# Head of a seven-product output stage: sums moved from GpSimd to VectorE, joint loads of y, loads of weights behind the last copy

## The chip, the cores and the metric

The kernel runs on one core of one Trainium2 chip. The metric is device time in microseconds for one execution; the time before is 2018.6 us, the median of three runs (2017.74 to 2028.34). The names of the engines in views and text: PE is TensorE, DVE is VectorE, ACT is ScalarE, POOL is GpSimd, SP is SyncE; SPq and ACTq are the DMA queues that SP and ACT issue on.

## The reference, cut to what matters

The kernel computes one layer of a hybrid backbone (a gated DeltaNet mixer and a windowed attention mixer) on 2048 latent tokens of width 1024, with 256 context tokens as a prefix. The change lies in its last step, the merge of the two branches and the output projection:

```python
def _merge(ya, yb, ga, gb, w_proj_a, w_proj_b, w_out):
    y = jax.nn.sigmoid(ga) * (ya @ w_proj_a) + jax.nn.sigmoid(gb) * (yb @ w_proj_b)
    return y @ w_out
...
    x = x + gate[:, None] * _merge(ya, yb, ga, gb, w_proj_a, w_proj_b, w_out)
```

`y` is 2048 x 1024, `w_out` is 1024 x 1024, the output is 2048 x 1024 in float32.

## The kernel before, in words

Everything is float32, and each matrix product is made of three passes: an operand is split into a high part of reduced precision (a copy by ACT, a CAST in the profile) and a low part (the operand less its high part, a subtraction on DVE or POOL), and PE adds high x high, low x high and high x low.

**The projections (`project`, `load_y`).** The tokens lie in four groups of 512. For each group the attention and DeltaNet outputs are loaded (`yr`, L1210), copied to `yh` by ACT (L1211) and their low parts `yl` made by DVE (L1212). Then, for each of eight slices m of the width, PE makes two products of 12 matmuls (`pps`, L1229 to L1231), DVE multiplies each by its gate (`ta`, `tb`, L1237, whose gates are loaded from `gasp` and `gbsp` into two buffers each), the two are added (L1239: POOL for the first three groups, DVE for the last) and the sum is stored to `ysp` (L1240) by SP. The last group is index 3. PSUM holds eight banks (`acc`), which go to whichever product comes next as they come free.

**The seven-product stage.** The output projection takes y in eight units of 256 tokens, each a 2 x 2 arrangement of blocks A11, A12, A21, A22 (A's first index is the half of 128 tokens, its second the half of 512 channels), and `w_out` in four quarters B11, B12, B21, B22 of 512 x 512. Each unit takes seven products in place of eight: P1 = A11 B11, P2 = A12 B21, P3 = S4 B22, P7 = S3 T3, P6 = S2 T2, P5 = S1 T1, P4 = A22 T4, with S3 = A11 - A21, S2 = A22 - S3, S4 = A12 - S2, S1 = S2 + A11 on the side of y, and on the side of the weights T3 = B22 - B12 (L1342), T2 = T3 + B11 (L1344), T1 = B22 - T2 (L1457) and T4 = B21 - T2 (L1474). Each product is 12 matmuls (L1434 to L1436). The sums overwrite an operand: T3 stands in B12's tile, T2 in B11's, T1 in B22's, T4 in B21's. Low parts then take over tiles that are done with: T2's that of B12, T1's that of B11, T4's that of B22.

PE's order is the list `seq`: for the first two units each product is made for both units in turn (P1 of unit 0, P1 of unit 1, P2 of unit 0, ...), since the weights' sums are being made then; from unit 2 on it goes unit by unit. Position k in `seq` is the loop's counter. For a position k the high part `ah` (L1319) is made by `his(k)` on ACT and the low part `al` (L1323) by `los(k)`, on DVE, or on POOL for P4. `split_lo` makes the weights' low parts (L1309, 128x2048, on DVE but for T4, which POOL makes).

**What sets the order.** Inside `manual_schedule` DVE, ACT, POOL (and PE in the second block) run in the order in which the code is written, each engine waiting in that order. DMAs are issued on ACT's queue (`adma`: the quarters of `w_out`, L1297, and the blocks of y, L1304) and on SP's (`dma`: x, the gate row `gbc`, the outputs), in order as well; a DMA issue waits until its buffer is free, and the completion semaphores, eight in number, are given to the DMAs of both queues in turn, so that an issue also waits for the earlier DMA on its own semaphore. `issue_after(last["yh", 2])` holds the first loads until the copy of the third y tile of group 3 has been issued; there are four such copies.

The outputs (`outputs(k)`, run one position behind the products) add products into `held` and `hold2` tiles on DVE (L1403 to L1425), `store` multiplies by the gate row (L1389) and adds x (L1390, POOL but for unit 7) and stores.

## Time and profile before

| what | value |
|---|---|
| median of 3 runs | 2018.6 us |
| profiled execution | 2021.32 us |
| its span, first to last instruction | 2019.4 us |
| PE busy | 1923.7 us (95%) |
| DVE busy | 1501.3 us (74%) |
| ACT busy | 807.4 us (40%) |
| POOL busy | 713.7 us (35%) |
| mean granted TensorE clock | 0.984 |

In the timelines a row gives start, duration, engine, line, operation, output<-inputs, shape, and how many alike are merged (x2). A bracket at the end gives how long the engine had been idle before and what released it. "issue" as releaser means that the engine's own queue was busy, with DMA issues for instance. In the rows of waits stand the waiting engine and line, what it waited for, and the total in us, how often, and the longest. Matmuls overlap: their starts are 0.23 us apart at full clock, whatever the duration shown.

### The profile page before, as it was taken

To read this page: it belongs to the slowest core of one execution; us is meant where nothing else is said; L and a number is where in the kernel's file an instruction comes from. 1 tells how busy PE (TensorE), PEld (TensorE's weight loads), DVE (VectorE), ACT (ScalarE), POOL (GpSimd) and SP (SyncE) were. 2 spreads that over 40 slices of the span, in tenths; PEclk is the share of its full clock that TensorE was granted. 3 is DMA by queue.
4 is the path that set the end of the run, shared out by engine and by line. 5 is a ranking of instruction groups with operands and counts; after the bars stand their busy time and mean duration, and the time that the engine had idled before them with its cause. 6 is when DMAs were issued, how large, how long until landed. Compare 5 with 4: busy or idle time off the path is not lost. (4 is left out here: it accounts for less than half of the span.)

```text
span 2019.4 us, 32107 instructions
## 1 busy us (share of the span) xinstructions
PE 1923.7 (95%) x10947; PEld 1611.3 (80%) x10947; DVE 1501.3 (74%) x2863; ACT 807.4 (40%) x1998; POOL 713.7 (35%) x776
## 2 busy tenths in 40 slices
PE   6999999989999999999999999999989999997898
PEld 3888888779998778787888888888778887875786
DVE  6979766667776999999677775536677778657667
ACT  5755545554443322111222232325665656432211
POOL 1742211224542211004222243324555444414675
PEclk8999999999999999999999999999999999998999
DMA  7552326755546633528977777673455645363444
GB/s 259 165 141 85 96 88 159 198 147 157 151 146 181 175 115 110 146 85 234 242 232 225 227 231 210 169 215 116 159 183 159 193 152 178 99 222 110 150 158 130
DMA packets 387831, 333.12 MB, mean 165 GB/s; under 512 B 84120, under 2 KB 307664, under 8 KB 387028
## 3 DMA queue, kind: packets, MB, share of 16 engines
q1 hardware_dynamic: 352244, 288.60, 49.5%
q10 hardware_dynamic: 35424, 42.48, 6.0%
q8 instruction: 87, 1.43, 0.3%
q14 instruction: 76, 0.62, 0.1%
HBM read 220.28 MB, written 109.13 MB: 163 GB/s over the span
## 5 line engine op out<-in xcount | busy, mean ns | idle before, releaser
L524 PE MATMUL rps<-hh,wh 128*128 128x512 f32 x768 | 308.7, 402 | 4.4 <-DVE rt L818 3.2
L526 PE MATMUL rps<-hh,wl 128*128 128x512 f32 x768 | 308.7, 402 | 0.0
L525 PE MATMUL rps<-hl,wh 128*128 128x512 f32 x768 | 307.1, 400 | 0.0
L563 DVE SCALAR_TENSOR_TENSOR cacc<-y,cw,cacc 128x512 f32<-128x512 f32 (+1 forms) x224 | 161.2, 741 | 22.8 <-ACT cacc L561 18.6
L524 PEld LDWEIGHTS rps<-hh,wh 128*128 128x128 f32 x768 | 145.3, 189 | 39.5 <-DVE rt L818 4.0
L524 PE MATMUL lps<-hh,wh 128*128 128x512 f32 (+1 forms) x448 | 171.5, 383 | 0.3 <-ACT y L634 0.3
L525 PEld LDWEIGHTS rps<-hl,wh 128*128 128x128 f32 x768 | 145.4, 189 | 32.6
L525 PE MATMUL lps<-hl,wh 128*128 128x512 f32 (+1 forms) x448 | 171.3, 382 | 0.0
L526 PE MATMUL lps<-hh,wl 128*128 128x512 f32 (+1 forms) x448 | 171.2, 382 | 0.0
L526 PEld LDWEIGHTS rps<-hh,wl 128*128 128x128 f32 x768 | 145.3, 189 | 32.4
L945 DVE TENSOR_TENSOR pl<-pt,ph 128x512 fp32r<-128x512 f32 x156 | 105.4, 685 | 44.4 <-ACT ph L943 43.7
L943 ACT CAST ph<-pt 128x512 fp32r<-128x512 f32 x156 | 90.2, 585 | 109.5 <-PE pt L941 77.0
L917 DVE CUSTOM_DVE_ANT_0 pr<-sc,band,sk 128x640 f32<-128x640 f32 (+1 forms) x128 | 106.6, 862 | 32.6 <-PE sc L913 16.6
L816 ACT ACTIVATE rt<-rps 128x512 f32<-128x512 f32 x96 | 57.2, 596 | 172.2 <-PE rps L526 155.1
L749 DVE TENSOR_TENSOR N<-N,btmp 128x62 f32<-128x62 f32 (+30 forms) x124 | 118.6, 957 | 3.0
L927 POOL TENSOR_SCALAR pr<-pr,sm 128x640 f32<-128x640 f32 (+1 forms) x128 | 99.3, 795 | 55.1 <-DVE sm L925 38.6
L747 DVE TENSOR_TENSOR btmp<-N 128x62 f32<-128x62 f32 (+30 forms) x124 | 115.6, 932 | 3.1
L919 ACT ACTIVATE pr<-pr,sm 128x640 f32<-128x640 f32 (+1 forms) x128 | 104.0, 815 | 20.0 <-DVE sm L917 20.0
L1229 PE MATMUL pps<-yh,wph 128*128 128x512 f32 x256 | 104.6, 412 | 5.2 <-ACT yh L1211 3.6
L245 POOL TENSOR_SCALAR wh<-wr 128x512 fp32r<-128x512 f32 x72 | 48.9, 693 | 169.7 <-PE lps L525 92.7
L246 DVE TENSOR_TENSOR wl<-wr,wh 128x512 fp32r<-128x512 f32 x120 | 90.9, 771 | 23.2 <-POOL wh L245 20.9
L1231 PE MATMUL pps<-yh,wpl 128*128 128x512 f32 x256 | 100.9, 396 | 0.0
(370 smaller groups left out, 5067.1 us busy)
## 6 DMA issues: line engine op xcount, KB each, us to landing
wr<-in_w_in_dram SPq DMA_DIRECT2D x120, 256.0 KB
kw<-Ksp SPq DMA_DIRECT2D x28, 384.0 KB
x<-vsp SPq DMA_DIRECT2D x36, 256.0 KB
k<-ksp SPq DMA_DIRECT2D x34, 256.0 KB
kT<-kTsp SPq DMA_DIRECT2D x34, 256.0 KB
wm<-in_w_mod_dram SPq DMA_DIRECT2D x16, 512.0 KB
xt<-in_x_dram SPq DMA_DIRECT2D x16, 512.0 KB
dtl<-Dsp SPq DMA_DIRECT2D x32, 256.0 KB
```

The source lines that it names most:

```text
L524: T.matmul(ps, lhsT=wh[:, k], rhs=xh[:, k], start=k == 0, stop=False)
L525: T.matmul(ps, lhsT=wh[:, k], rhs=xl[:, k], start=False, stop=False)
L526: T.matmul(ps, lhsT=wl[:, k], rhs=xh[:, k], start=False, stop=k == kt - 1)
L563: V.scalar_tensor_tensor(a, y[:, t:t + n], cw[:, m, t:t + 1], a, op0=ALU.mult, op1=ALU.add)
L747: V.tensor_tensor(tv, A[:, m + 1:, m].unsqueeze(2).to_broadcast([h1 + n, r, m]), A[:, m, 0:m].unsqueeze(1).to_broadcast([h1 + n, r, m]), o ...
L749: V.tensor_tensor(A[:, m + 1:, 0:m], A[:, m + 1:, 0:m], tv, op=ALU.add)
L917: V.tensor_tensor_reduce(s_, ps[:, o:768], band[:, b0:b0 + W + 256], -0.125, sk[:, 1, hd:hd + 1], ALU.add, ALU.min, sm[:, h, 1:2])
L919: S.activation(s_, s_, AF.Exp, scale=-1.0, bias=sm[:, h, 1:2], accum_out=sm[:, h, 2:3])
L927: G.tensor_scalar(p[:, h, :W + 256], p[:, h, :W + 256], sm[:, h, 3:4], 1.0, op0=ALU.mult, op1=ALU.mult)
L945: V.tensor_tensor(pl, pt, f32(ph), op=ALU.subtract)
L1229: T.matmul(ps, lhsT=wh[:, k, ms], rhs=hs[k], start=k == 0, stop=False)
L1231: T.matmul(ps, lhsT=wl[:, k, ms], rhs=hs[k], start=False, stop=k == 3)
```

## The change

1. The first loads of the stage (all four quarters of `w_out`, three blocks of y) are held until the fourth y copy of group 3 has been issued, where it was the third.
2. A21 and A22 of a unit, the two blocks of its second 128 tokens, come in one load of 512 KB into one tile, in place of two loads of 256 KB.
3. The sums S3, S2, S1 of units 0 and 1, the sums of weights T1 and T4, and T4's low part go from POOL to DVE, and DVE's instructions are written in the order in which PE needs them. Unit 2's S3, S2, S4 are made on DVE in one go at position 11, S1 on POOL.
4. The first output block of units 0 and 1 is held and stored at position 9; its multiplication by the gate is on POOL for unit 0 too.
5. From unit 2 on, the loads of the next unit are issued one position earlier (at i == 0).

The core of the diff:

```diff
         def load_quad(u, nm):
             gi, o = units[u]
-            r, c = int(nm[1]) - 1, int(nm[2]) - 1
+            if nm == "A2":
+                t = p4.tile([128, 8, 128], F32, name="yA2", tag=f"yA2{u % 2}")
+                adma(t, ysp[gi][:, :, o + 128:o + 256])
+                Y[u, "A21"], Y[u, "A22"] = t[:, 0:4], t[:, 4:8]
+                return
+            c = int(nm[2]) - 1
...
-            with tc.issue_after(last["yh", 2].ins):
+            with tc.issue_after(last["yh", 3].ins):
                 load_w("B11")
...
-            gp = V if u in (0, 7) else G
+            gp = V if u == 7 else G
...
-                store(u, "00", og, gp)
+                if u < 2:
+                    early[u] = og, G
+                else:
+                    store(u, "00", og, gp)
...
-            for q in ((0, "A21"), (0, "A22"), (1, "A12"), (1, "A21"), (1, "A22")):
+            for q in ((0, "A2"), (1, "A12"), (1, "A2")):
                 load_quad(*q)
...
             los(2)
-            s3(0)
-            s2(0, G)
             his(3)
             los(3)
             split_lo("B22", V)
-            s3(1)
-            s2(1, G)
+            s3(0, V)
+            s2(0, V)
             s4(0)
             his(4)
-            G.tensor_tensor(B["B22"], B["B22"], B["B11"], op=ALU.subtract)
             for k in range(len(seq) + 1):
                 u, i = divmod(k, 7)
-                if i == 1 and 2 <= u < 7:
-                    for nm in ("A11", "A12", "A21", "A22"):
+                if i == 0 and 2 <= u < 7:
+                    for nm in ("A11", "A12", "A2"):
                         load_quad(u + 1, nm)
                 if k + 4 < len(seq):
                     los(k + 4)
                 if k == 0:
                     S.copy(hi["T2"], B["B11"])
+                    s3(1, V)
+                    s2(1, V)
                     s4(1)
                 elif k == 1:
                     split_lo("T3", V, "B12")
-                    s1(0)
-                    s1(1)
-                elif k == 2:
+                elif k == 3:
                     split_lo("T2", V, "B11", "B12")
-                    G.tensor_tensor(B["B21"], B["B21"], B["B11"], op=ALU.subtract)
-                elif k == 3:
+                    V.tensor_tensor(B["B22"], B["B22"], B["B11"], op=ALU.subtract)
+                elif k == 4:
                     S.copy(hi["T1"], B["B22"])
-                elif k == 4:
-                    split_lo("T1", V, "B22", "B11")
+                    s1(0, V)
+                    s1(1, V)
+                    V.tensor_tensor(B["B21"], B["B21"], B["B11"], op=ALU.subtract)
                 elif k == 5:
                     S.copy(hi["T4"], B["B21"])
-                    split_lo("T4", G, "B21", "B22")
+                    split_lo("T1", V, "B22", "B11")
                 elif k == 7:
-                    for nm in ("A11", "A12", "A21"):
-                        load_quad(2, nm)
-                elif k == 8:
-                    load_quad(2, "A22")
+                    split_lo("T4", V, "B21", "B22")
+                    load_quad(2, "A11")
+                    load_quad(2, "A12")
+                elif k == 9:
+                    load_quad(2, "A2")
+                    for u in range(2):
+                        store(u, "00", *early[u])
+                elif k == 11:
+                    s3(2, V)
+                    s2(2, V)
+                    s4(2)
+                    s1(2, G)
```

**What it moves.** On DVE, in the head of the stage, the rows before from B22's low part on (`al` and `ah` are low and high parts, `s2` is S2, `yA12` turns into S4, `yA21` is S3):

```order
L1309 TENSOR_TENSOR B22l_19525<-B22_19481,B22h_19485 128x2048
L1366 TENSOR_TENSOR yA12_19498<-yA12_19498,s2_19556 128x512
L1323 TENSOR_TENSOR al_19522<-yA12_19498,ah_19521 128x512
L1366 TENSOR_TENSOR yA12_19538<-yA12_19538,s2_19562 128x512
L1323 TENSOR_TENSOR al_19524<-yA12_19538,ah_19523 128x512
L1309 TENSOR_TENSOR T3l_19526<-B12_19482,B12h_19486 128x2048
```

And now, to the same instruction (`yA2` is the joint tile, its first half turns into S3):

```order
L1314 TENSOR_TENSOR B22l_19525<-B22_19481,B22h_19485 128x2048
L1363 TENSOR_TENSOR yA2_19534<-yA11_19491,yA2_19534 128x512
L1368 TENSOR_TENSOR s2_19555<-yA2_19534 128x512
L1371 TENSOR_TENSOR yA12_19498<-yA12_19498,s2_19555 128x512
L1328 TENSOR_TENSOR al_19522<-yA12_19498,ah_19521 128x512
L1363 TENSOR_TENSOR yA2_19538<-yA11_19493,yA2_19538 128x512
L1368 TENSOR_TENSOR s2_19562<-yA2_19538 128x512
L1371 TENSOR_TENSOR yA12_19536<-yA12_19536,s2_19562 128x512
L1328 TENSOR_TENSOR al_19524<-yA12_19536,ah_19523 128x512
L1314 TENSOR_TENSOR T3l_19526<-B12_19482,B12h_19486 128x2048
```

S3 and S2 of both units stand on DVE in front of the S4 that needs them. On POOL, the stage began with

```order
L1358 TENSOR_TENSOR yA21_19534<-yA11_19491,yA21_19534 128x512
L1363 TENSOR_TENSOR s2_19556<-yA22_19536,yA21_19534 128x512
L1358 TENSOR_TENSOR yA21_19540<-yA11_19493,yA21_19540 128x512
L1363 TENSOR_TENSOR s2_19562<-yA22_19542,yA21_19540 128x512
L1457 TENSOR_TENSOR B22_19481<-B22_19481,B11_19479 128x2048
L1370 TENSOR_TENSOR yA11_19491<-s2_19556,yA11_19491 128x512
L1370 TENSOR_TENSOR yA11_19493<-s2_19562,yA11_19493 128x512
L1474 TENSOR_TENSOR B21_19480<-B21_19480,B11_19479 128x2048
```

and now begins with the low parts of P4 of units 0 and 1 and the held output blocks (`og`):

```order
L1328 TENSOR_TENSOR al_19708<-yA2_19534,ah_19707 128x512
L1328 TENSOR_TENSOR al_19725<-yA2_19538,ah_19724 128x512
L1394 TENSOR_TENSOR og_19638<-og_19638,gbc_19540 128x512
L1395 TENSOR_TENSOR xr_19542<-og_19638,xr_19542 128x512
L1394 TENSOR_TENSOR og_19661<-og_19661,gbc_19540 128x512
```

All of POOL's sums in the head are gone from its queue. On ACT, at the end of the projections, stood before

```order
L1211 CAST yh_19181<-yr_19183 128x512
L1297 DMA B11_19479<-in_w_out_dram 128x4x512
L1304 DMA yA11_19491<-ysp1_134 128x4x128
L1304 DMA yA11_19493<-ysp1_134 128x4x128
L1297 DMA B22_19481<-in_w_out_dram 128x4x512
L1297 DMA B12_19482<-in_w_out_dram 128x4x512
L1297 DMA B21_19480<-in_w_out_dram 128x4x512
L1304 DMA yA12_19498<-ysp1_134 128x4x128
L1211 CAST yh_19181<-yr_19187 128x512
```

and now, for ACT, with the copy of the last y tile first:

```order
L1211 CAST yh_19181<-yr_19183 128x512
L1211 CAST yh_19181<-yr_19187 128x512
L1297 DMA B11_19479<-in_w_out_dram 128x4x512
L1309 DMA yA11_19491<-ysp1_134 128x4x128
L1309 DMA yA11_19493<-ysp1_134 128x4x128
```

The last y copy (`yh` from `yr_19187`) stood behind the seven loads and stands ahead of them now.

More of the change, by code (lines that the diff above doesn't have):

```diff
@@ L1300, in load_quad @@
             gi, o = units[u]
-            r, c = int(nm[1]) - 1, int(nm[2]) - 1
+            if nm == "A2":
[4 more added lines that the diff above has]
+            c = int(nm[2]) - 1
             po = {(0, "A11"): el, (0, "A12"): er, (1, "A11"): er}.get((u % 2, nm), p4)
             Y[u, nm] = po.tile([128, 4, 128], F32, name=f"y{nm}", tag=f"y{nm}{u % 2}")
-            adma(Y[u, nm], ysp[gi][:, c * 4:c * 4 + 4, o + r * 128:o + r * 128 + 128])
+            adma(Y[u, nm], ysp[gi][:, c * 4:c * 4 + 4, o:o + 128])
         def split_lo(nm, eng, src=None, place=None):
@@ L1354, in _hybrid, with s3 @@
             hi[nm] = BH(hr, nm + "h")
-        def s3(u):
-            G.tensor_tensor(Y[u, "A21"], Y[u, "A11"], Y[u, "A21"], op=ALU.subtract)
+        def s3(u, eng):
+            eng.tensor_tensor(Y[u, "A21"], Y[u, "A11"], Y[u, "A21"], op=ALU.subtract)
             Y[u, "S3"] = Y[u, "A21"]
@@ L1367, in s4, with s1 @@
             Y[u, "S4"] = Y[u, "A12"]
-        def s1(u):
-            G.tensor_tensor(Y[u, "A11"], Y[u, "S2"], Y[u, "A11"], op=ALU.add)
+        def s1(u, eng):
+            eng.tensor_tensor(Y[u, "A11"], Y[u, "S2"], Y[u, "A11"], op=ALU.add)
             Y[u, "S1"] = Y[u, "A11"]
-        R, held = {}, {}
+        R, held, early = {}, {}, {}
         outs = [(u, q) for u, nm in seq for q in {"P2": ["00"], "P5": ["11", "01"], "P4": ["10"]}.get(nm, [])]
@@ L1469, in _hybrid @@
                     split_lo("T3", V, "B12")
[L1470 to L1472 removed]
+                elif k == 3:
                     split_lo("T2", V, "B11", "B12")
[L1474 to L1475 removed]
+                    V.tensor_tensor(B["B22"], B["B22"], B["B11"], op=ALU.subtract)
+                elif k == 4:
                     S.copy(hi["T1"], B["B22"])
[L1477 to L1478 removed]
+                    s1(0, V)
+                    s1(1, V)
+                    V.tensor_tensor(B["B21"], B["B21"], B["B11"], op=ALU.subtract)
                 elif k == 5:
                     S.copy(hi["T4"], B["B21"])
[L1481 removed]
+                    split_lo("T1", V, "B22", "B11")
                 elif k == 7:
[L1483 to L1486 removed]
+                    split_lo("T4", V, "B21", "B22")
[10 more added lines that the diff above has]
+                    s1(2, G)
                 if k + 6 < len(seq):
                     u, nm = seq[k + 6]
[L1489 to L1490 removed]
+                    if u > 2 and nm == "P2":
+                        s3(u, G)
                         s2(u, V)
[L1492 removed]
+                    elif u > 2 and nm == "P7":
                         s4(u)
[L1494 removed]
+                        s1(u, G)
                 if k + 5 < len(seq):
```

4 lines of the change are left out of this document (removed).

## The prediction

> **What bounds the kernel now.** The chain of work that ended last is short and only names the tail, so I began with the busy time by stage, then asked what TensorE (PE) waits for, then read the timelines of PE, DVE, ACT and POOL between 1789 and 1911 us. By stage (us, then busy time and instruction count of PE, PEld, DVE, ACT, POOL, then granted clock, DMA share, GB/s):
>
> ```profile
> 1840.00:1860.00 20.00, 12.91 (x38) 8.48 (x38) 17.19 (x8) 8.00 (x10) 15.05 (x5) 0.83 0.22 75
> 1860.00:1880.00 20.00, 17.93 (x70) 14.24 (x70) 13.78 (x11) 3.56 (x4) 11.85 (x6) 0.91 0.30 93
> 1880.00:1900.00 20.00, 15.32 (x59) 12.44 (x60) 16.63 (x23) 4.56 (x8) 10.53 (x7) 0.83 0.37 118
> 1900.00:1920.00 20.00, 20.00 (x89) 16.24 (x88) 14.09 (x18) 5.72 (x11) 12.93 (x9) 1.00 0.61 186
> ```
>
> From 1900 on PE does 89 matmuls in 20 us and never rests: 0.23 us for one, 2.8 us for a product of 12. In the 60 us before, it did 38 + 70 + 59 = 167, work of 38 us. About 22 us of the head are waiting or a lowered clock. What PE waited for there, and where:
>
> ```profile
> PE P L1434 <- ACT ah L1319: 6.9, 3, 4.5
> PE P L1434 <- DVE hold L1406: 5.5, 1, 5.5
> PE P L1436 <- DVE al L1323: 3.7, 3, 3.0
> PE P L1435 <- DVE B21l L1309: 2.1, 1, 2.1
> ```
> ```profile
> 1827.24 0.39 PE L1434 MATMUL P<-B11h,ah 128*128 128x512 f32 x1
> ...
> 1835.25 0.50 PE L1435 MATMUL P<-B21l,ah 128*128 128x512 f32 x1 [2.08 <-DVE B21l L1309]
> ...
> 1851.98 0.79 PE L1434 MATMUL P<-B22h,ah 128*128 128x512 f32 x1 [4.49 <-ACT ah L1319]
> ...
> 1861.23 0.78 PE L1436 MATMUL P<-B12h,al 128*128 128x512 f32 x1 [2.97 <-DVE al L1323]
> ...
> 1884.67 0.77 PE L1434 MATMUL P<-T4h,ah 128*128 128x512 f32 x1 [5.51 <-DVE hold L1406]
> ...
> 1892.10 0.40 PE L1434 MATMUL P<-B11h,ah 128*128 128x512 f32 x1
> ...
> 2011.14 0.40 PE L1436 MATMUL P<-T4h,al 128*128 128x512 f32 x1
> ```
>
> The first product of the stage starts at 1827.24, the first of unit 2 at 1892.10: 64.9 us for 14 products that are 39.2 us of work, 25.7 us lost. From there to 2011.54 PE is the bound.
>
> **Why the waits are there.** DVE and POOL get in each other's way:
>
> ```profile
> 1840.58 2.29 DVE L1309 TENSOR_TENSOR B22l<-B,B22h 128x2048 fp32r<-128x2048 f32 x1
> 1842.78 0.69 DVE L1366 TENSOR_TENSOR yA<-yA,s 128x512 f32<-128x512 f32 x1
> 1844.15 0.69 DVE L1323 TENSOR_TENSOR al<-yA,ah 128x512 fp32r<-128x512 f32 x1 [0.68 <-ACT ah L1319]
> 1846.28 5.00 DVE L1366 TENSOR_TENSOR yA<-yA,s 128x512 f32<-128x512 f32 x1 [1.44 <-POOL s L1363]
> ...
> 1852.87 3.37 DVE L1309 TENSOR_TENSOR T3l<-B,B12h 128x2048 fp32r<-128x2048 f32 x1
> 1856.17 5.02 DVE L1323 TENSOR_TENSOR al<-yA,ah 128x512 fp32r<-128x512 f32 x1
> ...
> 1883.23 0.69 DVE L1363 TENSOR_TENSOR s<-yA,yA 128x512 f32<-128x512 f32 x1 [9.42 <-POOL yA L1358]
> ```
> ```profile
> 1846.19 4.53 POOL L1457 TENSOR_TENSOR B<-B,B 128x2048 f32<-128x2048 f32 x1
> ...
> 1854.05 6.58 POOL L1474 TENSOR_TENSOR B<-B,B 128x2048 f32<-128x2048 f32 x1
> ...
> 1873.23 5.06 POOL L1309 TENSOR_TENSOR T4l<-B,T4h 128x2048 fp32r<-128x2048 f32 x1
> ...
> 1881.95 1.26 POOL L1358 TENSOR_TENSOR yA<-yA,yA 128x512 f32<-128x512 f32 x1
> ```
>
> A DVE sum of 128x512 takes 0.69 us when POOL rests and 5.00 when it starts 0.09 us after POOL's 4.53-us sum: it ends 0.56 us after POOL does, so it stood still for that whole instruction. PE's 4.49 us at 1851.98 (unit 1's S4), its 2.97 us at 1861.23, and its 5.51 us at 1884.67 follow from this: the last because DVE stood 9.42 us at unit 2's S2, waiting for POOL's S3 behind T4's low part, with the additions that free PE's banks (L1406) queued behind it.
>
> **The change, part by part.**
>
> *The last y copy before the loads of w_out.* Now the copy to yh sits on ACT behind seven DMA issues:
>
> ```profile
> 1789.61 0.62 ACT L1211 CAST yh<-yr 128x512 fp32r<-128x512 f32 x1 [5.07 <-DMA yr<-ybsp]
> 1789.62 0.42 ACTq L1297 DMA_DIRECT2D B<-in_w_out_dram  x1
> ...
> 1795.60 0.62 ACT L1211 CAST yh<-yr 128x512 fp32r<-128x512 f32 x1 [5.37 <-issue]
> ```
> ```profile
> 1796.27 0.97 PE L1229 MATMUL pps<-yh,wph 128*128 128x512 f32 x3 [1.45 <-ACT yh L1211]
> ```
>
> Its load was issued with the one that landed at 1789.61, some 0.4 us later, so I estimate the copy at 1790.3, five us earlier, and the weights' loads 0.7 us later. PE's 1.45 us go: the projections end and the products begin at 1825.8. But this by itself is worth nothing, because the next thing PE needs, the low part of B21, does not move with it:
>
> ```profile
> 1831.42 0.68 DVE L1237 SCALAR_TENSOR_TENSOR tb<-tb,pps 128x512 f32<-128x512 f32 x1
> 1832.02 3.18 DVE L1309 TENSOR_TENSOR B21l<-B,B21h 128x2048 fp32r<-128x2048 f32 x1
> ```
>
> DVE reaches B21l only after the last gate product, whose gates arrive through two buffers, load by load. I keep 1832.0 as its start; loads of weights that are 0.7 us later can push it, DVE's slightly regrouped gate products can pull it: 1831 to 1834.
>
> *Fewer loads of y.* Now five loads, the last two stuck in ACT's queue until the store of the last gates has finished; ACT's copy for unit 1's P2 waits behind them:
>
> ```profile
> 1826.08 2.91 ACTq L1304 DMA_DIRECT2D yA<-ysp  x3
> 1832.94 6.33 ACTq L1304 DMA_DIRECT2D yA<-ysp  x2
> 1839.32 0.62 ACT L1319 CAST ah<-yA 128x512 fp32r<-128x512 f32 x1 [14.29 <-DMA ysp<-ta]
> ```
>
> Three loads are left and, by the first row, three pass in 2.91 us. The copy then comes at about 1830 to 1832, ahead of PE's need (1837). The joint load of 512 KB is wanted by DVE only at 1838; it is hidden by B21l and B22l.
>
> *All sums on DVE.* From B21l to the low part that unit 1's P6 needs, DVE's order holds six instructions of 128x2048 (B21l, B22l, T3l, T2l, and the two sums of weights, the latter from POOL) and 19 of 128x512 (eleven of them as before, eight sums of units 0 and 1 that join, all but two from POOL). A large one takes 2.2 us from start to start (1840.58 to 1842.78), a small one 0.6:
>
> ```profile
> 1800.27 1.29 DVE L1323 TENSOR_TENSOR al<-yA,ah 128x512 fp32r<-128x512 f32 x2
> ```
>
> 6 x 2.2 + 19 x 0.6 = 24.6 us; four sums that need the one before add about 0.1 each; twice DVE waits for ACT's copy of a sum it has just made, 0.68 us each (row at 1844.15). Together 26.4 us: 1832.0 + 26.4 = 1858.4. PE meanwhile: B21l ready at 1834.3 (2.29 us as for B22l, no POOL beside it), P2 ends at 1840, P3 waits about 0.8 us for the copy of S4 and runs to 1847.5, P7 follows T3l (1847.3) to 1853, P6 of unit 0 to 1856.5, P6 of unit 1 waits for its low part until 1858.4. After that ten more matmuls of P6 (2.3 us) and P5, P4 of both units (11.2 us): unit 2 begins at 1872.0, against 1892.1. Gain 20.1 us.
>
> Is anything late in those last 11 us? T1l (2.2 us), two low parts, T4l (2.2 us): DVE is done with T4 at 1864.2, PE wants it at 1866.4. L1406's successor follows at once and frees the bank; the 5.51-us wait goes. POOL has only P4's two low parts by then, and the held outputs come behind them.
>
> *Held outputs, unit 2's sums on DVE, the later loads one product earlier.* Seven to ten small instructions on engines with room (DVE 14.09, POOL 12.93 of 20 us in the row of 1900); PE's unit takes 19.9 us there ((2011.54 - 1892.10) / 6). I cost these at nothing; the cover at unit 2's P7 is thin:
>
> ```profile
> 1883.85 0.68 DVE L1406 TENSOR_TENSOR hold<-P,hold 128x512 f32<-128x512 f32 x1
> ...
> 1896.18 1.78 DVE L1323 TENSOR_TENSOR al<-yA,ah 128x512 fp32r<-128x512 f32 x1
> ```
>
> From the first addition to P7's low part DVE needs 14.1 us now (1883.85 to 1897.96); with two sums more it needs about 15.3, from 1864.2 to 1879.5, and PE comes to that product 8.4 us after unit 2 begins, at 1880.4. If the cover fails, 1 to 2 us are lost once.
>
> *The clock.* PE's longest gap will be 1831.4 to 1834.3, 2.9 us. After a gap of 2.08 us its first matmul took 0.50 us, after one of 2.97 us 0.78, and the stage 1860 to 1880, which holds that gap, was granted 0.91: 9% of 20 us, 1.8 us. That is the price of such a gap if all of it counts; PE waits for DVE in P3 and P6 anyway, so I take 1.0 off. [...]
>
> **Sum.** 20.1 - 1.0 = 19 us. The profiled execution's 2021.32 us (span 2019.4) would become 2002.3. It ran 2.7 us above the median of 2018.6; against that median, 1999.6. No gap at all in the head would give 27 us (25.7 + 1.45): 1991.5.
>
> **Rivals.**
>
> *DVE stays slow.* If the large instructions keep 3.2 to 3.4 us (rows at 1832.02 and 1852.87), six times 1.1 = 6.6 us are added: gain 12.5, 2006. For it: DVE is the chain. Against it: each of those rows has POOL beside it, and B22l without POOL took 2.29. [...] Chance 0.14.
>
> *The gain moves into the wait for B21l.* The last gates arrive a round later, where a round is the store of two results and the load of two more gates into their buffers:
>
> ```profile
> 1820.57 0.69 DVE L1237 SCALAR_TENSOR_TENSOR ta<-ta,pps 128x512 f32<-128x512 f32 x1 [0.81 <-DMA ta<-gasp]
> ...
> 1830.82 0.69 DVE L1237 SCALAR_TENSOR_TENSOR ta<-ta,pps 128x512 f32<-128x512 f32 x1 [0.85 <-DMA yA<-ysp]
> ```
>
> That is 10.25 us: gain 8.9, 2009.7. For it: B21l is queued behind the second of them and PE waits for B21l. Against it: the loads in front move by 0.7 us only. Chance 0.09.
>
> *Slower.* The joint load of a later unit may be issued only when POOL has made the low part of P4 two units before, since both halves share a buffer; ACT's copies for P5, P4 and the next P1 queue behind that issue. If POOL is later than ACT at that point, every unit from 3 to 7 stops. Over 3.8 us per unit (19 / 5) the kernel is slower; at 6 us it is 2029.6. Against it: POOL's work per unit is as before, 12.93 of 20 us. Chance 0.05.
>
> **The numbers.** Forecast 0.72: 1994 to 2004. Half a per cent (10 us) is about what a measurement of this kernel tells from no change: the forecast and the slow DVE lie beyond it, 0.86; the wait for B21l within, 0.09; slower 0.05. The range 1994 to 2008 takes in the forecast and the slow DVE.
>
> **What would show it.** Right: no PE wait over 3 us after 1836; B21l in 2.3 us; unit 2's P1 near 1872; the last y copy before the first load of w_out; no POOL instruction between 1790 and 1862. Wrong: large DVE instructions above 3 us, B21l starting after 1835, or PE waits that return in units 3 to 7.

## The result and the profile after

| | before | after |
|---|---|---|
| median of 7 runs each | 2019.33 us (2017.74 to 2028.34) | 2011.05 us (2008.36 to 2014.61) |
| ratio of the times | | 0.9949, 95% interval 0.9929 to 0.9968 |
| profiled execution, its span | 2021.32 us, 2019.4 | 2014.61 us, 2012.8 |

In this measurement the change is worth 8.3 us, not 19. The forecast of 1999.6 us was wrong, and 2011.05 lies above the range. A second measurement (e7 below), in 10 runs, gave 0.995 (0.9933 to 0.9966), about 10 us.

Runs of one kernel scatter by several us, and much of that arises ahead of the stage. I therefore measure inside one execution, from a mark upstream that the change does not touch: the first low part of y of the last quarter, on DVE, in the profile of before and then of after.

```profile
1772.67 1.47 DVE L1212 TENSOR_TENSOR yl<-yr,yh 128x512 fp32r<-128x512 f32 x2 [0.43 <-ACT yh L1211]
```
```profile
1776.54 1.47 DVE L1212 TENSOR_TENSOR yl<-yr,yh 128x512 fp32r<-128x512 f32 x2 [0.43 <-ACT yh L1211]
```

From there to the end of the span it is 246.73 us before and 236.26 after: 10.5 us gained. (The profiled run of after came 3.9 us late to the mark, so the spans differ by 6.6 only.)

Busy time by stage of after, columns as in the prediction:

```profile
1840.00:1860.00 20.00, 18.57 (x70) 14.24 (x71) 18.49 (x19) 5.69 (x8) 0.00 (x0) 0.87 0.28 94
1860.00:1880.00 20.00, 18.05 (x77) 13.96 (x77) 18.78 (x19) 7.65 (x9) 9.23 (x6) 1.00 0.22 68
1880.00:1900.00 20.00, 17.37 (x74) 13.37 (x73) 14.50 (x19) 4.43 (x8) 15.99 (x11) 1.00 0.67 216
1900.00:1920.00 20.00, 19.49 (x84) 15.24 (x82) 14.48 (x17) 4.43 (x8) 13.49 (x10) 1.00 0.53 165
1960.00:1980.00 20.00, 19.61 (x84) 15.25 (x83) 14.47 (x17) 4.43 (x8) 13.49 (x10) 1.00 0.50 156
```

The head is denser: 70 and 77 matmuls where there were 38 and 70. But from 1900 on PE does 84 in 20 us, not 89. The waits of PE in after say who keeps it:

```profile
PE P L1444 <- DVE al L1328: 6.3, 9, 1.6
PE P L1443 <- DVE B21l L1314: 5.7, 1, 5.7
```

The starts of P1 of units 0, 2, 3 and 7 on PE in after, with the wait for the low part of B21:

```profile
1829.80 0.39 PE L1442 MATMUL P<-B11h,ah 128*128 128x512 f32 x1
...
1841.43 0.79 PE L1443 MATMUL P<-B21l,ah 128*128 128x512 f32 x1 [5.69 <-DVE B21l L1314]
...
1845.49 0.40 PE L1443 MATMUL P<-B21l,ah 128*128 128x512 f32 x1
...
1879.44 0.40 PE L1442 MATMUL P<-B11h,ah 128*128 128x512 f32 x1
...
1902.11 0.40 PE L1442 MATMUL P<-B11h,ah 128*128 128x512 f32 x1
...
1983.72 0.40 PE L1442 MATMUL P<-B11h,ah 128*128 128x512 f32 x1
```

and of before, for units 3, 4, 6 and 7 (unit 2's, at 1892.10, stands in the prediction):

```profile
1911.48 0.40 PE L1434 MATMUL P<-B11h,ah 128*128 128x512 f32 x1
...
1930.82 0.40 PE L1434 MATMUL P<-B11h,ah 128*128 128x512 f32 x1
...
1969.89 0.40 PE L1434 MATMUL P<-B11h,ah 128*128 128x512 f32 x1
...
1990.31 0.40 PE L1434 MATMUL P<-B11h,ah 128*128 128x512 f32 x1
```

In after units 0 and 1 take 49.6 us together (64.9 before), unit 2 takes 22.67, and units 3 to 6 take (1983.72 - 1902.11) / 4 = 20.40 us each. Before, units 2 and 3 took 19.38 and 19.34, units 4 and 5 19.54 on average, unit 6 20.42. Unit 2 starts 16.5 us nearer to the mark, and 6.1 us of that are given back behind it.

What gives it back shows on DVE and POOL. Every S2 on DVE waits about 5 us for POOL's S3. In the profile of before, two of its rows, for units 3 and 4:

```profile
1907.46 0.69 DVE L1363 TENSOR_TENSOR s<-yA,yA 128x512 f32<-128x512 f32 x1 [5.07 <-POOL yA L1358]
...
1927.86 0.69 DVE L1363 TENSOR_TENSOR s<-yA,yA 128x512 f32<-128x512 f32 x1 [5.06 <-POOL yA L1358]
```

And one whole period in after, DVE and then POOL:

```profile
1900.91 0.69 DVE L1368 TENSOR_TENSOR s<-yA 128x512 f32<-128x512 f32 x1 [6.34 <-POOL yA L1363]
...
1911.54 1.28 DVE L1394 TENSOR_TENSOR hold<-hold,gbc 128x512 f32<-128x512 f32 x2
...
1921.29 0.69 DVE L1368 TENSOR_TENSOR s<-yA 128x512 f32<-128x512 f32 x1 [5.08 <-POOL yA L1363]
```
```profile
1912.30 3.37 POOL L1395 TENSOR_TENSOR xr<-hold,xr 128x512 f32<-128x512 f32 x2 [4.94 <-DMA xr<-in_x_dram]
1915.63 1.75 POOL L1394 TENSOR_TENSOR hold<-hold,gbc 128x512 f32<-128x512 f32 x1
1917.45 1.28 POOL L1395 TENSOR_TENSOR xr<-hold,xr 128x512 f32<-128x512 f32 x1
1918.70 1.32 POOL L1328 TENSOR_TENSOR al<-yA,ah 128x512 fp32r<-128x512 f32 x1
1919.97 1.29 POOL L1363 TENSOR_TENSOR yA<-yA,yA 128x512 f32<-128x512 f32 x1
...
1932.68 3.37 POOL L1395 TENSOR_TENSOR xr<-hold,xr 128x512 f32<-128x512 f32 x2 [4.94 <-DVE hold L1394]
```

The first POOL row names a load of x as what ended its wait, but POOL starts 0.08 us after DVE's first gated output, and after the same 4.94 us, as in the next period, whose row names that output; in the four later periods of after it is always named.

This is a ring. DVE goes from S2 to the gated outputs of P5 (11.4 us). POOL adds x to them, finishes output 10, makes P4's low part and then, last, the next unit's S3 (9.0 us with the hand-over). Only then can DVE make the next S2. It is 20.4 us round in both kernels, and PE needs 19.34 for a unit. So the ring, not PE, sets the end, before as well as after; e1, e2 and e3 below test this. Before, S2 of unit 3 stood 4.0 us ahead of PE's P1 of that unit; the ring ate 1 us of this lead per unit, and PE did not feel it until unit 5. After, the lead is 1.2 us from unit 3 on, and PE waits in every unit. What reached the end is therefore how far S2 of unit 3 moved: 134.79 us after the mark before, 124.37 after, 10.4 us, the whole gain.

### The profile page after: what moved, and what is told of

It reads as the page before. It is cut to its first block, busy times and chain, and to the rows that moved or that the text cites. A ratio compares the mean times of both kernels' runs of the same rounds, so it can differ in the third digit from the quotient of the medians.

```text
span 2012.8 us, 32096 instructions
## 1 busy us (share of the span) xinstructions
PE 1924.7 (96%) x10947; PEld 1611.6 (80%) x10947; DVE 1501.4 (75%) x2871; ACT 807.2 (40%) x1998; POOL 689.5 (34%) x768
## 5 line engine op out<-in xcount | busy, mean ns | idle before, releaser
L919 ACT ACTIVATE pr<-pr,sm 128x640 f32<-128x640 f32 (+1 forms) x128 | 104.0, 815 | 19.8 <-DVE sm L917 19.8
```

Source lines behind the costliest of these rows:

```text
L919: S.activation(s_, s_, AF.Exp, scale=-1.0, bias=sm[:, h, 1:2], accum_out=sm[:, h, 2:3])
```

## The experiments

The five columns in the middle are us from the mark in each kernel's own profile. Then come the median time, or the one time where there was a single execution, and the ratio to the kernel before on the same chip, with its interval. Kernels e9 to e12 ran on another chip than e1 to e8, where the kernel before took 2016.55 us (median of 11 runs), so their times are not to be set against the others.

| kernel | B21's low part starts | unit 2 starts on PE | S2 of unit 3 | unit 3 starts on PE | end | time, us | ratio |
|---|---|---|---|---|---|---|---|
| before | 59.35 | 119.43 | 134.79 | 138.81 | 246.73 | 2019.33 | 1 |
| after | 62.55 | 102.90 | 124.37 | 125.57 | 236.26 | 2011.05 | 0.9949 (0.9929-0.9968) |
| e1_s3_early | 58.76 | 99.12 | 116.67 | 125.34 | 230.31 | 2002.03 | 0.9928 (0.9904-0.9953) |
| e2_loads_back | 61.82 | 102.16 | 123.61 | 124.82 | 235.36 | 2011.38 | - |
| e3_before_s3 | 58.47 | 120.40 | 130.93 | 139.80 | 244.69 | 2015.43 | 0.9980 (0.9965-0.9995) |
| e4_gates_late | 51.21 | 96.01 | 117.46 | 118.66 | 229.36 | 2003.81 | 0.9931 (0.9909-0.9953) |
| e5_both | 51.41 | 95.99 | 113.60 | 121.56 | 227.15 | 2003.03 | 0.9925 (0.9901-0.9949) |
| e6_best | 51.13 | 98.94 | 116.96 | 121.52 | 226.43 | 1997.87 | 0.9899 (0.9878-0.9920) |
| e7_after_again | 61.82 | 102.15 | 123.64 | 124.84 | 235.61 | 2008.45 | 0.9950 (0.9933-0.9966) |
| e8_copy_only | 61.07 | 121.74 | 136.16 | 141.11 | 248.12 | 2020.46 | 1.0004 (0.9990-1.0018) |
| e9_a2_behind | 59.54 | 101.23 | 122.69 | 123.89 | 234.57 | 2002.08 | - |
| e10_pool_sums | 62.20 | 110.21 | 128.05 | 129.59 | 239.91 | 2019.30 | - |
| e11_not_held | 60.52 | 103.49 | 123.41 | 124.62 | 235.30 | 2012.68 | - |
| e12_best2 | 51.35 | 101.32 | 115.67 | 120.70 | 225.68 | 2001.47 | 0.9919 (0.9899-0.9938) |

Two columns subtracted tell the story. In the nine kernels that keep S3 at the end of POOL's round (before, after, e2, e4, e7 to e11) it is 111.75 to 111.97 us from S2 of unit 3 to the end, whatever PE did. In four of the five that move S3 forward (e1, e3, e6, e12) it is 104.89 to 104.98 us from PE's start of unit 3 to the end, and 105.59 in e5, where that unit's first matmuls start 0.43 us apart, not 0.23.

**S3 out of the ring** (e1).

```diff
                     for nm in ("A11", "A12", "A2"):
                         load_quad(u + 1, nm)
+                    s3(u + 1, G)
...
                     if u > 2 and nm == "P2":
-                        s3(u, G)
                         s2(u, V)
```

> The changed kernel, but S3 of units 3 to 7 (POOL) stands right behind the unit's three loads, so in POOL's queue it is ahead of the two multiplications and additions for output 10 and of al for P4, and no longer the last thing behind all outputs of the unit before. Theory A (the end is set by a loop of DVE and POOL: S2 on DVE, 11.4 us of DVE up to the gated outputs, 9 us of POOL that end with S3, and S2 again, 20.4 us a unit, while PE needs 19.36): S3 leaves the end of the loop, the five starts of S2 are no longer 20.4 us apart, units 3 to 6 of PE fall from 20.4 to about 19.4 us, and the time falls by 4 to 6 us against the changed kernel's 2011 (2005 to 2007). Rival B (units 3 to 7 are slow because the joint load of A21 and A22 and the loads one product earlier disturb ACT's and PE's queues): the loads are untouched, units stay at 20.4 us, time 2011 within 1.5. Rival C (PE itself is the bound, as the prediction said): no change either, 2011.

The S2 after the first follow 18.1 us apart, and units 3 to 6 of PE take 19.32 to 19.48 us: the ring is no longer the bound. POOL and DVE in this experiment:

```profile
1895.81 3.37 POOL L1395 TENSOR_TENSOR xr<-hold,xr 128x512 f32<-128x512 f32 x2 [3.24 <-DVE hold L1394]
1899.14 1.74 POOL L1363 TENSOR_TENSOR yA<-yA,yA 128x512 f32<-128x512 f32 x1
1900.84 1.29 POOL L1394 TENSOR_TENSOR hold<-hold,gbc 128x512 f32<-128x512 f32 x1
```
```profile
1900.91 1.77 DVE L1368 TENSOR_TENSOR s<-yA 128x512 f32<-128x512 f32 x1 [1.18 <-POOL yA L1363]
...
1918.99 1.77 DVE L1368 TENSOR_TENSOR s<-yA 128x512 f32<-128x512 f32 x1 [1.17 <-POOL yA L1363]
```

S3 comes ahead of output 10, and DVE's wait falls from 5.1 to 1.2 us. Some of it is lost in unit 2, which takes 26.2 us: P4's low part is later on POOL (1885.74 to 1887.48), and PE waits 1.86 us for it, and then runs at a granted clock of 0.50, in the rows shown further down, under the hardware. The time is 2002.03 us, below the 2005 to 2007 expected. From the mark the end is 5.3 us earlier than in the second profile of after (e7), but 3.1 of these are an earlier low part of B21, which the edit does not touch: S3 itself gave 2.2 us net of unit 2.

**The loads as they were** (e2): units 3 to 7 load at the second product, A21 and A22 in two DMAs.

```diff
-                if i == 0 and 2 <= u < 7:
+                if i == 1 and 2 <= u < 7:
...
-                adma(t, ysp[gi][:, :, o + 128:o + 256])
+                for c in (range(2) if u > 2 else ()):
+                    adma(t[:, c * 4:c * 4 + 4], ysp[gi][:, c * 4:c * 4 + 4, o + 128:o + 256])
+                if u <= 2:
+                    adma(t, ysp[gi][:, :, o + 128:o + 256])
```

> The changed kernel, but units 3 to 7 load at the unit's second product again and A21 and A22 in two DMAs, as in the kernel before; the head is untouched. Rival B (loads): units 3 to 6 of PE return from 20.4 to 19.4 us, time some 4 us below the changed kernel's. Theory A (DVE-POOL loop): S2 stays 20.4 us apart and PE's units 3 to 6 stay at 20.4 us, time 2011 within 2.

Units 3 to 6 take 20.36 to 20.41 us and S2 stays 20.35 to 20.49 apart. The loads have nothing to do with it; this also disposes of the prediction's rival in which the joint load stops units 3 to 7.

**S3 out of the ring in the kernel before** (e3).

```diff
-                if i == 1 and 2 <= u < 7:
+                if i == 0 and 2 <= u < 7:
                     for nm in ("A11", "A12", "A21", "A22"):
                         load_quad(u + 1, nm)
+                    s3(u + 1)
...
                     if u > 1 and nm == "P2":
-                        s3(u)
+                        if u == 2:
+                            s3(u)
```

> The kernel before, but units 3 to 7 load at the unit's first product and S3 of those units stands right behind the loads on POOL, as in the first experiment. Theory A: before, DVE and POOL had a lead of some 4 us over PE at unit 2 which the loop ate at 1 us a unit; only units 5, 6 and 7 (19.73 and 20.42 us) were held by it, so PE's units all become 19.35 us and 1.4 to 2.5 us go: 2017 (about 2 us below the kernel before). Rival C (PE is the bound, the slower units 5 and 6 were PE's clock): no change, 2019 within 1. Rival B: earlier loads make units slower than 19.4 us, the time grows by up to 4 us.

Units 2 to 6 take 19.40, 19.33, 19.34, 19.49, 19.45; from the mark 2.0 us go (3.0 from the start of unit 2, which came 1.0 us later), by the ratio 4.0 (1.0 to 7.1). So the kernel before was held by the ring too, though only at its end.

**The last gate products behind B22's low part** (e4). In the part left out, the `tb` gates of these two products also get two buffers of their own, and `late_gate` makes the products, their sum and its store.

```diff
-                V.scalar_tensor_tensor(t, t, 1.0, ps, op0=ALU.add, op1=ALU.mult)
-                us.append(t)
+                if not (gi == 3 and m >= 6):
+                    V.scalar_tensor_tensor(t, t, 1.0, ps, op0=ALU.add, op1=ALU.mult)
+                us.append((t, ps) if gi == 3 and m >= 6 else t)
+            if gi == 3 and m >= 6:
+                late.append((us, m))
+                continue
...
             los(2)
+            split_lo("B22", V)
+            late_gate()
             his(3)
             los(3)
-            split_lo("B22", V)
+            late_gate()
```

> The changed kernel, but the last two of the eight gate products of the fourth quarter (their multiplications, addition and store; the loads stay where they were) stand on DVE behind the low part of B21, unit 0's low part for P2 and the low part of B22, and no longer ahead of them. If the gate loads that land late are what held DVE's chain (low part of B21 began 2.7 us later than predicted, PE waited 5.7 us for it): PE's wait for the low part of B21 goes, DVE's chain to the low part of T4 ends some 5 us earlier, the first S2 of unit 3 too, and as the rest is a chain of DVE and POOL the whole gain reaches the end: 2006 (4 to 6 us below the changed kernel). Rival (the loads of A12 and A2 for the two units bound the head as well, or PE does): PE waits as long for al of unit 1's P2 or for S4, gain under 2 us.

The low part of B21 starts 10.6 to 11.3 us earlier and PE no longer waits for it. The gate products now cost DVE their time inside the chain, so S2 of unit 3 is 6.2 to 6.9 us earlier, and the end by 6.2 to 6.9 us also, with the ring still at 20.4. The time, 2003.81 us, is below the 2006 expected.

**Both** (e5): the edits of e1 and e4.

> The changed kernel with the edits of the first and the fourth experiment together (S3 of units 3 to 7 right behind the loads; the last two gate products behind the low part of B22). If the two causes are separate, their gains add: against the last upstream mark the first S2 of unit 3 comes some 6 us earlier than in the changed kernel and S2 then follows every 18 to 19.4 us, not every 20.4; time about 1999 (0.990 of the kernel before). But unit 2 loses some of it, as in the first experiment, where PE waited 1.9 us for al of unit 2's P4, which then stands behind S3 on POOL. If the lead that the gates give is only eaten again further on (one limit behind both), the time stays at the 2002 to 2004 of the two single edits.

From the mark the end is 2.2 us below e4's, just what S3 gave in e1 by itself, so by the profiles the two causes are separate; and as there, unit 2 loses most of what S3 could give (25.6 us). The time, 2003.03 us where about 1999 was expected, is no lower than that of the single edits: 2 us are within the scatter of the runs.

**And P4's low parts on DVE from unit 2 on** (e6).

```diff
-            (G if nm == "P4" else V).tensor_tensor(A[k][1], Y[u, OPS[nm][0]], f32(A[k][0]), op=ALU.subtract)
+            (G if nm == "P4" and u < 2 else V).tensor_tensor(A[k][1], Y[u, OPS[nm][0]], f32(A[k][0]), op=ALU.subtract)
```

> As the experiment with both edits, and the low part al for P4 of units 2 to 7 is made by DVE, no longer by POOL. DVE waits some 2.4 us for S3 in each unit there, so the 0.7 to 1.2 us per unit are free for it; PE's wait of 1.9 us for al of unit 2's P4 should go, and unit 2 of PE falls from 26.2 us (first experiment) to about 22. Time 2 to 4 us below the experiment with both edits, 1995 to 1998 (0.988 to 0.990). Rival: POOL's outputs block DVE's extra operations with two inputs in SBUF, DVE becomes the bound and nothing is gained on top.

Unit 2 falls to 22.58 us as expected. The head of this profile is 3 us longer than that of e5, since unit 1's A12 landed later, so that from the mark it gains 0.7 only. The time is 1997.87 us (1992.74 to 2004.22), 0.9899 of the kernel before: the lowest ratio of all, with an interval that overlaps those of e1, e4, e5 and e12, and lower than that of the changed kernel in e7 (0.9950), whose interval it does not touch.

**The changed kernel again** (e7).

> The changed kernel again, unaltered, on the same chip as the others of this call. Its profile is to show what belongs to the program and what to one run: the 20.4 us between two S2 and 32.3 us from the start of the low part of B21 to the end of the low part of T4 should return within 0.1; the wait of PE for the low part of B21 (5.7 us in the first profile, 0.3 us in the first experiment, which has the same head) and the upstream marks may differ by some us. Ratio to the kernel before 0.993 to 0.997.

S2 stands 20.38 to 20.51 us apart, the chain takes 32.39 us, PE again waits 5.7 us for the low part of B21. The gain from the mark is 11.1 us.

**Only the y copy** (e8), in the kernel before.

```diff
-            with tc.issue_after(last["yh", 2].ins):
+            with tc.issue_after(last["yh", 3].ins):
```

> The kernel before with one part of the change: the first loads of weights wait for the fourth copy of y (the last), not for the third. The prediction says that the y copy comes 3 us earlier, PE's wait of 1.45 us for it goes, and that this alone is worth nothing, because DVE's and POOL's chain from the low part of B21 sets the end: ratio 1.000 within 0.001. Rival (the end hangs on PE through the head): 1.5 us faster, 0.9992. Rival (later weight loads delay the chain): up to 3 us slower.

No gain: 1.0004. PE starts the stage 1.35 us nearer to the mark (53.22, 54.57), but the low part of B21 starts 1.7 us farther and PE waits 4.7 us for it, not 2.1.

**Why B21's low part is late** (e9).

```diff
-            for q in ((0, "A2"), (1, "A12"), (1, "A2")):
-                load_quad(*q)
+            load_quad(1, "A12")
...
             los(2)
             his(3)
+            for q in ((0, "A2"), (1, "A2")):
+                load_quad(*q)
             los(3)
```

> The changed kernel, but in the head ACT issues the loads of A21 and A22 of units 0 and 1 (512 KB each) behind the cast of unit 1's A12, and A12's load ahead of them. Theory: the low part of B21 begins late because the first 512-KB load is issued ahead of the last two loads of gates (0.6 us ahead in the changed kernel's second profile, where PE waits 5.7 us for the low part of B21; 2.2 us behind them in the first experiment, where PE waits 0.3 us). Then here the wait falls to under 2 us and the low part of B21 begins 58 to 60 us after the upstream mark (the start of the last quarter's first low part of y), not 61.8 to 62.6; part of it may be lost again, since S3 of unit 0 waits for a later A21. Rival (the gate loads land late for another reason, such as the weight loads behind the last copy): wait 5 us or more, 61.8 again.

The start is at 59.54 us, as expected, but PE still waits 3.4 us, not under 2; and the chain up to the end of T4's low part takes 33.7 us, 1.3 more, since S3 of unit 1 waits 1.26 us for its load (S3 of unit 0 does not wait). One half of the theory holds. The rows that I went by are those of ACT's queue, SP's queue and DVE in after:

```profile
1828.64 0.63 ACTq L1303 DMA_DIRECT2D yA<-ysp  x1
```
```profile
1829.62 2.48 SPq L1236 DMA_DIRECT2D ta<-gasp  x2
```
```profile
1835.45 0.69 DVE L1237 SCALAR_TENSOR_TENSOR ta<-ta,pps 128x512 f32<-128x512 f32 x1 [3.65 <-DMA ta<-gasp]
```

and the same three in e1, where PE waited 0.3 us:

```profile
1819.85 0.59 ACTq L1303 DMA_DIRECT2D yA<-ysp  x1
```
```profile
1817.67 2.25 SPq L1236 DMA_DIRECT2D ta<-gasp  x2
```
```profile
1822.27 0.69 DVE L1237 SCALAR_TENSOR_TENSOR ta<-ta,pps 128x512 f32<-128x512 f32 x1 [2.68 <-DMA ta<-gasp]
```

In after the first load of y is issued 1.0 us ahead of the last two gate loads, in e1 2.2 us behind them; the first gate product that needs them comes 5.8 us after their issue in after and 4.6 in e1. That is 1.2 us; the gate loads just ahead of these are later too, DVE waited 4.2 us for them in after and 2.8 in e1. The order divides the ten profiles in which the gates stand ahead of B21. Where the load was behind (before, e1, e3, by 2.0 to 2.9 us) the low part starts 58.5 to 59.4 us after the mark; where it was ahead (after, e2, e7 to e11), 59.5 to 62.6. ACT's load waits for the last projection of PE (the cast of A12 ahead of it, at 1826.97 in after, is released by it), and PE is earlier when it no longer waits for the y copy (by 1.35 us in e8). The code does not fix the order: e1 has the head of after and came out the other way. That the order does it is thus borne out by ten profiles and half an experiment, not shown on its own; that B21's low part waits for the gates is shown by e4.

**The two sums of weights on POOL again** (e10).

```diff
-                    V.tensor_tensor(B["B22"], B["B22"], B["B11"], op=ALU.subtract)
+                    G.tensor_tensor(B["B22"], B["B22"], B["B11"], op=ALU.subtract)
...
-                    V.tensor_tensor(B["B21"], B["B21"], B["B11"], op=ALU.subtract)
+                    G.tensor_tensor(B["B21"], B["B21"], B["B11"], op=ALU.subtract)
```

> The changed kernel, but the two 128x2048 subtractions that make T1 and T4 are POOL's again, in their old places. The prediction priced what DVE gains by having no POOL operation beside it at 26.4 us from the low part of B21 to that of unit 1's P6. If that is right, POOL's two sums (about 5 us each in the kernel before) block DVE's operations with two inputs in SBUF for 4 us each, more than the 2.28 us each that DVE saves, and DVE waits for T1 and T4: from the start of the low part of B21 to the end of the low part of T4 36 to 42 us, not 32.3, and unit 2 of PE starts 4 to 9 us later. Rival (POOL's sums run beside DVE for free): 28 us, unit 2 starts 2 to 4 us earlier.

36.4 us, and unit 2 starts 7.3 to 8.1 us later. POOL and DVE there:

```profile
1846.01 4.79 POOL L1479 TENSOR_TENSOR B<-B,B 128x2048 f32<-128x2048 f32 x1 [57.88 <-DVE B22l L1314]
1850.77 4.94 POOL L1484 TENSOR_TENSOR B<-B,B 128x2048 f32<-128x2048 f32 x1
```
```profile
1846.42 4.94 DVE L1368 TENSOR_TENSOR s<-yA 128x512 f32<-128x512 f32 x1
1851.39 4.87 DVE L1371 TENSOR_TENSOR yA<-yA,s 128x512 f32<-128x512 f32 x1
```

Two DVE sums of 0.69 us take 4.9 each. Of the 7 to 8 us lost at unit 2 half is back at the end: S2 of unit 3 is 3.7 to 4.4 us later than in the two profiles of after, and the end 3.7 to 4.3.

**The first outputs not held** (e11): `store` at once for units 0 and 1.

```diff
-                if u < 2:
-                    early[u] = og, G
-                else:
-                    store(u, "00", og, gp)
+                store(u, "00", og, gp)
```

> The changed kernel, but the outputs 00 of units 0 and 1 are multiplied, added and stored by POOL at once, not held until the loads of unit 2. The prediction took the holding at nothing. If POOL's four operations (5.9 us in the changed kernel) block DVE wherever they stand, the low part of T4 ends 2 to 5 us later after that of B21 begins (34 to 37 us, not 32.3), and unit 2 of PE, which takes 22.7 us with them in it, takes 20 to 21: the end moves by less than 2 us. Rival (holding is what makes the head short): the end 3 to 5 us later against the upstream mark. Rival (holding costs the 3 us of unit 2 and is worth nothing in the head): 2 to 3 us earlier.

36.1 us for the chain and 21.1 for unit 2; the end is 0.3 to 1.0 us nearer to the mark, but with a low part of B21 that starts 1.3 to 2.0 us earlier, so holding is worth 1 us. POOL's outputs lengthen DVE's sums here too (two of 128x512 take 3.45 us at 1866.48, against 1.28 at 1867.98 in after), and POOL is blocked itself: this multiplication takes 1.29 us alone (at 1895.69 in after, where DVE is idle). DVE beside it:

```profile
1857.66 5.06 POOL L1394 TENSOR_TENSOR og<-og,gbc 128x512 f32<-128x512 f32 x1 [71.17 <-DVE og L1408]
```
```profile
1857.50 0.68 DVE L1328 TENSOR_TENSOR al<-s,ah 128x512 fp32r<-128x512 f32 x1
1858.10 1.28 DVE L1375 TENSOR_TENSOR yA<-s,yA 128x512 f32<-128x512 f32 x2
1859.30 2.28 DVE L1481 TENSOR_TENSOR B<-B,B 128x2048 f32<-128x2048 f32 x1
```

**All of P4's low parts on DVE, the loads of x later** (e12), on top of e6.

```diff
-            (G if nm == "P4" and u < 2 else V).tensor_tensor(A[k][1], Y[u, OPS[nm][0]], f32(A[k][0]), op=ALU.subtract)
+            return V.tensor_tensor(A[k][1], Y[u, OPS[nm][0]], f32(A[k][0]), op=ALU.subtract)
...
-            for q in ((0, "A2"), (1, "A12"), (1, "A2")):
+            for q in ((1, "A12"), (0, "A2"), (1, "A2")):
                 load_quad(*q)
             gbc = p4.tile([128, D], F32, name="gbc")
-            dma(gbc, gsp.to_broadcast([128, D]))
-            for j in range(4):
-                load_x(j)
...
-            los(3)
+            with tc.issue_after(los(3).ins):
+                dma(gbc, gsp.to_broadcast([128, D]))
+                for j in range(4):
+                    load_x(j)
             late_gate()
```

> The best so far (S3 right behind the loads, the last two gate products behind the low part of B22, P4's low parts on DVE from unit 2 on) and three things more: P4's low parts of units 0 and 1 on DVE too, so that POOL makes none; the load of A12 of unit 1 ahead of the 512-KB loads; and the loads of the gates of the outputs and of the first four tiles of x behind the low part of unit 1's P2. In the best so far unit 1's A12 took 8.6 us from issue to landing beside these loads and DVE stood 3.2 us for it; POOL's two low parts took 3.47 us beside DVE and held the load of unit 2's A21 and A22 by 2.5 us. Expected: from the first unit to unit 2 43 us (46.2 before this), unit 2 of PE about 21 (22.6), the others 19.4; from the upstream mark to the end 222 to 225 us (226.4), time 1992 to 1996. Rival (DVE is the bound of the head, and al of P4 only loads it more): no gain, 1998 within 2.

Unit 2 takes 19.38 us, better than expected, but units 0 and 1 take 49.0, not 43. In both, DVE is the bound of the head:

```profile
1840.00:1860.00 20.00, 17.45 (x71) 12.80 (x71) 19.25 (x18) 9.79 (x12) 7.91 (x3) 1.00 0.03 12
1860.00:1880.00 20.00, 18.35 (x73) 14.32 (x72) 19.86 (x24) 5.18 (x9) 8.80 (x5) 0.91 0.54 165
```

DVE is busy for 19.25 and 19.86 of 20 us. Against e6 what one gains the other loses, and the end from the mark differs by 0.8 us: no gain on top.

## Why the prediction was wrong, step by step

- **"From there to 2011.54 PE is the bound": this step failed.** PE was busy for all of the 20 us from 1900 on, and I took that for a bound on every unit to the end. The ring of DVE and POOL was slower (20.4 against 19.34 us a unit) and only hidden by a lead of 4 us. My 19.9 us for PE's unit was a mean over units of 19.33 to 20.42 us and the last one, of 21.2: the drift that told of it stood in the trace, and so did a wait of some 5.06 us for POOL at every S2 from unit 3 on. The change moved unit 2 on PE by 16.5 us but S2 of unit 3 by 10.4, and that one counts. Cost: 6.1 us; PE shows 3.3 of them in unit 2, the rest in units 3 to 5. That the ring sets the pace is shown by e1, e2 and e3.
- **"I keep 1832.0 as its start" (1831 to 1834): off by 3.2 us,** 62.55 after the mark, not 59.35. I put the lateness to weights' loads 0.7 us later (0.8 measured); the loads of y that come earlier, the likelier cause (e9, not shown on its own), were not in the sum. The rival "the gain moves into the wait for B21l" was right in its place, but with a third of its price and another cause; that its 2009.7 us lie close to the measured 2011.05 is chance.
- **The y copy: its mechanism right, "worth nothing" right in the time** (e8: 1.0004). The last copy came 17.75 us after the mark, as I estimated (1790.3 is 17.6). But the loads of y then came ahead of the last two gate loads, in seven of the eight profiles that have this order and the gates ahead of B21.
- **"All sums on DVE": right.** From the start of B21's low part to the end of T4's:

```profile
1839.09 2.28 DVE L1314 TENSOR_TENSOR B21l<-B,B21h 128x2048 fp32r<-128x2048 f32 x1
...
1869.18 2.28 DVE L1314 TENSOR_TENSOR T4l<-B,T4h 128x2048 fp32r<-128x2048 f32 x1
```

  32.4 us, predicted 32.2 (1832.0 to 1864.2); from the same start to unit 2 on PE 40.35 us, predicted 40.0 and 1.0 for the clock. Large instructions take 2.28 us, so "DVE stays slow" is out. POOL does nothing from 1787.8 to 1870.42. Undoing a part (e10) costs what POOL's blocking says: 36.4 us, with two sums of 0.69 us at 4.94 and 4.87.
- **Fewer loads of y:** the copy for unit 1's P2 came 61.4 us after the mark, 2 to 4 later than I said. DVE reached its low part right behind the low part of B21, so this cost nothing of its own.
- **Held outputs and unit 2's sums, "at nothing": wrong by 3.3 us in unit 2,** though "1 to 2 us lost once" was the bound I gave if the cover failed. From the first addition to P7's low part DVE took 19.8 us (1871.39 to 1891.16), not 15.3, with five sums of 128x512 at 1.73 to 1.77 us beside POOL, and PE waited for the low parts of S4 and S3:

```profile
1886.56 0.50 PE L1444 MATMUL P<-B22h,al 128*128 128x512 f32 x1 [1.03 <-DVE al L1328]
...
1891.22 0.51 PE L1444 MATMUL P<-B12h,al 128*128 128x512 f32 x1 [1.60 <-DVE al L1328]
```

  These are the 3.3 us of the first step, not further ones. PE's two waits are not the ring's doing, since e1 breaks the ring and keeps them (1.01 and 1.61 us). But with the ring as it is, taking them away would not by itself move the end: in e10 unit 2 takes 19.38 us without them, and it is still 111.9 us from S2 of unit 3 to the end. e11 puts 1.5 us of the 3.3 to the held outputs. Whether these pay depends on the head: there they save 3.7 us of DVE's chain.
- **The clock:** the gap was 5.7 us, not 2.9; the ten matmuls behind it took 4.1 us (1841.43 to 1845.49), at a granted clock of 0.50 from 1841 to 1845, where ten take 2.3. So 1.8 us, not 1.0.
- **A slip without consequence:** by 24 matmuls of 0.23 us P3 would have ended at 1846.4, not 1847.5; nothing hung on it, since unit 1's P6 was to wait for DVE until 1858.4.
- **The sum:** 19.1 - 3.2 (late start) - 6.1 (lost behind the start of unit 2) + 0.65 (unit 2 after that start, clock included) = 10.45 us, which is what the profiles give from the mark. The medians of the timed runs differ by 8.3 us, and the interval of the ratio allows 6.5 to 14.3.

## What to carry to other kernels

An engine that is busy without a break need not be the bound (here PE, 20.00 of 20 us from 1900 on in before): take two marks of the same step a unit apart, on every engine, and compare the periods; a ring of two engines that is slower than the busy one eats its lead until it shows (20.4 against 19.34 us a unit). Count a change of the head at the instruction on which the steady part hangs (here S2 of unit 3), not where the busy engine starts. And where a wait is taken from one engine, its later DMA issues can come ahead of those of another queue (by 1.0 us in after): look at what they then delay.

## What the runs showed of the hardware

The clock fell after a shorter wait than the 2.97 us that the prediction went by. In e1 PE waited 1.86 us for P4's low part, and the matmuls then started 0.43 us apart, not 0.23:

```profile
1887.54 0.64 PE L1444 MATMUL P<-T4h,al 128*128 128x512 f32 x1 [1.86 <-POOL al L1328]
1887.98 0.63 PE L1442 MATMUL P<-T4h,ah 128*128 128x512 f32 x1
```

The granted clock there, in stretches of 2 us of e1 (busy time and instructions of PE, clock, DMA share, GB/s), and in before right behind its wait of 2.08 us for the low part of B21:

```profile
1888.00:1890.00 2.00, 2.00 (x6) 0.50 0.46 136
...
1892.00:1894.00 2.00, 2.00 (x10) 1.00 1.05 330
```
```profile
1836.00:1838.00 2.00, 2.00 (x9) 1.00 0.41 145
```

It was halved in e1, where two more waits of 1.01 and 1.61 us lay in the 15 us ahead, and not in before, so the length of the last wait alone does not decide; what does is not shown.

Two engines held each other up. In e10 a DVE sum of 0.69 us took 4.94 us beside a POOL sum of 4.79 and ended 0.56 us behind it; the next took 4.87 beside one of 4.94 and ended 0.55 us behind. In e11 it was POOL that stood, and not for one instruction only: its 1.3-us multiplication took 5.06 us, while DVE went through four sums of two tiles without a break (1857.50 to 1861.58), and ended 1.14 us behind the last of them. DVE's sums from PSUM were not lengthened: in after, `hold<-P,hold` took 0.68 and 0.67 us at 1886.42 and 1887.02 beside two POOL additions (3.37 us together, from 1884.29), where `al<-yA,ah`, a difference of two SBUF tiles, took 1.77 at 1884.73, not 0.68.
